# Outputs of the last two passes of each MoE layer combined by TensorE from SBUF; the overflow branch ahead of the passes; one comparison per pass index

## The chip, the core and the metric

The kernel runs on one core of a Trainium2 chip. Its five engines each work through a queue of their own: TensorE (PE, with its weight loads shown apart as PEld), VectorE (DVE), ScalarE (ACT), GpSimd (POOL) and SyncE (SP). Transfers run on 16 DMA engines and are issued from SP's and ACT's queues, and from POOL's queue where rows are picked by an index (indirect). The metric is the device time of one execution in microseconds.

## The reference

Two layers of a transformer over 256 latent and 256 context rows of width 1024. Each layer is attention, then a mixture of experts (MoE); the change touches the MoE and the lines around it. Cut to that:

```python
def moe(h, ...):                       # 16 experts in 4 groups, 2 experts per row
    s = jax.nn.sigmoid(h @ router_w); sel = s + router_bias
    ...                                # best group by its two best, then the top 2 of it
    w = take(s, idx); w = w / sum(w)
    act = silu(h @ w_gate[e]) * (h @ w_up[e]) * gates
    return sum_e act @ w_down[e]

x = layer_norm(ALPHA * x + g1 * attention(...), ln1_g, ln1_b)
y = moe(modulate(x, sh2, sc2), ...)
x = layer_norm(ALPHA * x + g2 * y, ln2_g, ln2_b)
```

Layer 0 does this for both streams (4 tiles of 128 rows), layer 1 for the latent rows alone (2 tiles). The output is the latent stream. All data are fp32.

## The kernel before

The MoE (`moe`) works in **passes**. A pass is a block of 128 row slots that belong to one to four experts (`unit_passes`: 11 passes in layer 0, 8 in layer 1). Routing on DVE gives each row two slots, one for each of its experts. The normalized rows `hx` are written to the memory table H; for each pass `route_index` builds a one-hot table `roh` on DVE, PE turns it into 128 row numbers `ridx`, and POOL fetches these rows from H (`xb<-H,ridx`). Then, per pass: PE turns the rows (`xbp`), `gate_up` multiplies them by gate and up weights (`pgu<-egu,xT`), `act` applies the activation (ACT `th`, DVE `ac`, PE `acp`, ACT `acT`), `down` gives the pass's output in PSUM (`y<-edn,acT`), and `rows_out` copies it to `yo` (DVE and ACT) and writes it to the memory table Y through ACT's queue. `down` of a pass stands one pass behind its `gate_up`.

Experts' weights are 3 MB each; SP loads them (`weight`, L1747) in pieces of 0.5 and 1 MB into pools of 11, 4 and 8 buffers, in the order of the passes. Which experts follow is read from DVE's table `metai`, except for two experts of layer 0 (table `early`) and the first group of layer 1, which are loaded ahead of the end of the routing.

At the end of a layer the rows come together. The **last** pass's output stays in PSUM, is multiplied by the gate vector g2 (`gated`, L1970, `ylast`) and is picked for each tile by a matmul with a one-hot table that carries the router's weights (`pcomb<-ylast,arena`, two matmuls a tile, each two rows of the trace). All other passes' outputs are picked from Y by POOL (`y_gather`, `yg<-Y,yslot`, two a tile), summed with the router's weights (`y_sum`: ACT L1875, DVE L1876), multiplied by g2 on POOL (`gate`, L1923), added to the residual (`add`, DVE L1963), and joined with `pcomb` (`combine`, DVE L1882). Behind the joins come the layer norm, and in layer 0 the first input projection of layer 1 (`pw`), whose weights `W1` are split in a high part (ACT CAST `whi<-wraw`, L1752) and a low part (POOL `wlo`, L1755 and L1759).

Rows beyond an expert's slots take the **overflow branch** (`tc.If(nov > 0)`, L1817), which stands behind `gate_up` of the second-to-last pass. With this data it is not taken. Each engine reads the flag and branches. On the way past it, SP waits until all transfers issued so far have landed, and raises the counters on which later reuses of the branch's buffers wait.

What sets the order on an engine is the order in which the code emits instructions, with priorities; inside `with self.ordered(last)` (the end of a layer) the order is as written.

Of the kernel before, what the change touches and what calls it, by code (L numbers as in the profile page):

```python
# [85 lines left out]
def shape_constants():  # L86
# [22 lines left out]
    route = np.zeros((DEPTH, 472), np.float32)  # L109
    for l in range(DEPTH):  # L110
        route[l, 0:256] = (e[None, :] < e[:, None]).reshape(-1)
        route[l, 256:384] = k
        route[l, 384:400] = e
        route[l, 400:408], route[l, 408:416] = slot_tables(l)
        route[l, 432:448] = 32 * e
        route[l, 448:452] = 4 * g
        route[l, 452:456] = g
        route[l, 456:472] = e % 4
# [10 lines left out]
NOROW = OVER + 5 * P  # L129
# [25 lines left out]
class Net:  # L155
# [160 lines left out]
    def consts2(self):  # L316
# [25 lines left out]
        self.Y = self.dr.tile([NOROW + P, D], F32, name="Y")  # L342
# [198 lines left out]
    def w_half(self, l, segs, h, wide=False):  # L541
# [660 lines left out]
    def out_proj(self, l, xs, tiles):  # L1202
# [18 lines left out]
        with self.ordered():  # L1221
            for n, k in enumerate(toks):
                p = toks[n - 1] if n else None
                self.out_half(k, W, 0, "AB")
                if n:
                    self.rows_turn(p)
                    self.rows_affine(p, 0)
                    self.rows_scale(p)
                    if n > 1:
                        self.route_gate(toks[n - 2])  # L1230
                    self.rows_affine(p, 1)
                    self.rows_sums(p, 3)
                    if n == 3:
                        self.route_choose(0)
                    if n == T - 1:
                        self.rows_scale(p)
                self.out_half(k, W, 0, "CD")
                self.rows_residual(k, 0)
                if n:
                    if n < T - 1:  # L1240
                        self.rows_scale(p)
                    self.rows_modulate(p)
                    if n == 3:
                        self.route_gates(0)
                    if n == T - 1:
                        self.rows_shift(p)
# [4 lines left out]
                if n == 3:  # L1251
                    self.route_early()
# [22 lines left out]
            if T == 4:  # L1275
                run[1]()
            self.rows_shift(end)
# [165 lines left out]
    def route_start(self, T):  # L1443
# [3 lines left out]
        k = self.small.tile([P, 216], F32, name="rk", bufs=1)  # L1447
        src = self.I["k_route"][self.l:self.l + 1, :]
        self.nc.scalar.dma_start(k, src[:, 256:472].to_broadcast([P, 216]))
        self.nc.scalar.dma_start(self.arena[:, 0:256], src[:, 0:256].to_broadcast([P, 256]))  # L1450
        self.iota, self.iota16, self.m32 = (k[:, a:b] for a, b in ((0, 128), (128, 144), (176, 192)))
        self.tab8 = k[:, 144:160].rearrange("p (a b) -> p a b", a=2)
# [709 lines left out]
```

## Time and profile before

| | |
|---|---|
| median of 3 runs | 1018.45 us (1015.17 to 1018.92) |
| the profiled execution | 1018.93 us, its span 1017.2 us |
| busy share of the span | PE 82%, DVE 56%, ACT 33%, POOL 20% |
[...]
| memory traffic | 231.55 MB, mean 228 GB/s |
| layer 0: passes and end | 400 to 620 us |
| layer 1: passes and end | 852 to 1017 us |

Times in rows are from the span's start. A row gives an instruction or several alike in a run (`xN`), its length, and in brackets how long its engine had been idle before it and what ended the idle time. SPq and ACTq are the queues' own DMA issues. A window's PEclk is the granted TensorE clock as a share of full speed; DMA is the mean busy share of the 16 DMA engines.

### The profile page before, as it was taken

The page shows a single profiled execution, that of the slowest core. Times are in us where ns is not written, and L with a number is a line of the kernel's source. Part 1 is how long each engine was busy: PE and PEld are TensorE (multiplying, and loading weights), DVE is VectorE, ACT ScalarE, POOL GpSimd, SP SyncE. Part 2 cuts the span into 40 slices and gives each one's busy share as a digit, 9 for nine tenths or more (in the row PEclk, how much of TensorE's full clock was granted, in tenths as well). Part 3 has the DMA queues.
Part 4 walks back from the last instruction along what each step waited for, and adds up shares of the span by engine and source line. Part 5 has one row for each costly group of instructions (what it writes and reads, how often), then busy time and mean ns, then how long its engine had stood idle before and what let it go on. Part 6 is the DMA issues. An engine that isn't in the chain of part 4 may idle for free. (4 is left out here: it accounts for less than half of the span.)

```text
span 1017.2 us, 12760 instructions
## 1 busy us (share of the span) xinstructions
PE 839.1 (82%) x4268; PEld 454.3 (45%) x4268; DVE 564.6 (56%) x1540; ACT 332.2 (33%) x775; POOL 203.3 (20%) x207
## 2 busy tenths in 40 slices
PE   4899999999899964699997348899997995897871
PEld 2476555545356732233332115665663673333320
DVE  4466776667485687523212198687776669320115
ACT  2243554535353210011111227555555520110101
POOL 1422110003230111100000384322235011100003
PEclk9999999999999985799999868999998997899986
DMA  9863666464624187999997642244525287999953
GB/s 341 291 232 115 214 210 225 133 237 135 243 89 171 42 291 267 388 327 401 366 400 257 221 161 83 83 166 120 161 90 159 83 289 259 345 391 402 395 205 119
DMA packets 131738, 231.55 MB, mean 228 GB/s; under 512 B 10192, under 2 KB 91696, under 8 KB 127568
## 3 DMA queue, kind: packets, MB, share of 16 engines
q1 hardware_dynamic: 116352, 186.84, 52.5%
q10 hardware_dynamic: 10992, 28.07, 7.7%
q0 software_dynamic: 4320, 15.73, 4.2%
q8 instruction: 37, 0.61, 0.2%
q14 instruction: 37, 0.30, 0.1%
HBM read 216.40 MB, written 17.89 MB: 230 GB/s over the span
## 5 line engine op out<-in xcount | busy, mean ns | idle before, releaser
L1785 PE MATMUL pgu<-egu,xT 128*32 128x512 f32 (+2 forms) x752 | 163.5, 623 | 16.7 <-DMA egu<-in_exp_w_gate_dram 6.5
L264 PE MATMUL pw<-whi,xhi 128*128 128x512 f32 (+1 forms) x224 | 94.5, 423 | 4.8 <-ACT xhi L476 4.0
L1038 ACT ACTIVATE P<-S,nm 128x512 f32<-128x512 f32 (+1 forms) x120 | 73.2, 614 | 76.8 <-DVE nm L1027 56.4
L1785 PEld LDWEIGHTS pgu<-egu,xT 128*32 128x32 f32 (+2 forms) x752 | 49.1, 132 | 106.5 <-issue 104.9
L266 PE MATMUL pw<-whi,xlo 128*128 128x512 f32 (+1 forms) x224 | 90.3, 406 | 3.9 <-DVE xlo L527 3.4
L265 PE MATMUL pw<-wlo,xhi 128*128 128x512 f32 (+1 forms) x224 | 90.3, 404 | 0.0
L1793 DVE SCALAR_TENSOR_TENSOR ac<-th,pgu 128x256 f32<-128x256 f32 x19 | 8.0, 420 | 134.7 <-ACT th L1791 134.7
L1807 PE MATMUL y<-edn,acT 128*32 128x512 f32 (+2 forms) x376 | 73.2, 617 | 6.6 <-ACT acT L1799 6.6
L1027 DVE TENSOR_REDUCE nm<-S 128x1 f32<-128x512 f32 (+1 forms) x120 | 68.4, 595 | 15.5 <-PE S L1000 11.0
L264 PEld LDWEIGHTS pw<-whi,xhi 128*128 128x128 f32 x224 | 43.2, 193 | 32.3 <-issue 16.2
L1682 POOL DMA_INDIRECT xb<-H,ridx x18 | 17.5, 972 | 191.8 <-DVE roh L1671 71.8
L365 PE MATMUL adaacc<-adaw,cst 128*32 128x512 f32 x256 | 53.8, 605 | 0.0
L254 POOL TENSOR_TENSOR wolo<-woraw,wohi 128x512 fp32r<-128x512 f32 x32 | 41.0, 1309 | 48.9 <-ACT wohi L253 48.7
L266 PEld LDWEIGHTS pw<-whi,xlo 128*128 128x128 f32 x224 | 43.0, 192 | 14.0 <-DVE xlo L527 4.7
L1068 PE MATMUL PTp<-ident,P 128*128 128x128 f32 x320 | 46.6, 277 | 2.9 <-DVE P L1056 2.5
L265 PEld LDWEIGHTS pw<-wlo,xhi 128*128 128x128 f32 x224 | 42.9, 191 | 9.9 <-issue 1.6
L1068 PEld LDWEIGHTS PTp<-ident,P 128*128 128x128 f32 x320 | 36.0, 141 | 24.3 <-issue 15.7
L1791 ACT ACTIVATE th<-pgu 128x256 f32<-128x256 f32 x19 | 7.3, 383 | 121.2 <-PE pgu L1785 84.6
L1807 PEld LDWEIGHTS y<-edn,acT 128*32 128x32 f32 (+2 forms) x376 | 23.1, 129 | 49.0 <-issue 32.7
L1975 PE MATMUL pcomb<-ylast,arena 128*128 128x512 f32 x24 | 20.0, 984 | 29.7 <-DVE ylast L1970 29.7
L264 PE MATMUL pwo<-wohi,oT 128*128 128x512 f32 x96 | 38.9, 405 | 0.7 <-ACT oT L258 0.7
L1075 ACT COPY PT<-PTp 128x512 f32<-128x512 f32 (+1 forms) x60 | 30.9, 514 | 22.6 <-PE PTp L1068 19.1
(412 smaller groups left out, 1580.6 us busy)
## 6 DMA issues: line engine op xcount, KB each, us to landing
adaw<-in_w_ada_dram SPq DMA_DIRECT2D x32, 1024.0 KB
egu<-in_exp_w_gate_dram SPq DMA_DIRECT2D x64, 512.0 KB
egu<-in_exp_w_up_dram SPq DMA_DIRECT2D x64, 512.0 KB
edn<-in_exp_w_down_dram SPq DMA_DIRECT2D x26, 1024.0 KB
adaw<-in_w_ada_dram SPq DMA_DIRECT2D x32, 512.0 KB
wraw<-in_w_in_dram SPq DMA_DIRECT2D x20, 512.0 KB
Y<-yo ACTq DMA_DIRECT2D x17, 512.0 KB
woraw<-in_w_out_dram SPq DMA_DIRECT2D x8, 1024.0 KB
```

The costliest lines, as they stand in the source:

```text
L254: eng.tensor_sub(lo[:, s], src[:, s], hi[:, s].bitcast(F32))
L264: mm(out, a[0], b[0], start=start, stop=False)
L265: mm(out, a[0], b[1], start=False, stop=False)
L266: return mm(out, a[1], b[0], start=False, stop=stop)
L365: self.nc.tensor.matmul(acc[32 * j:32 * j + 32, :], self.cst[:, k if row is None else row, :], t[:, j, :], start=(k == 0), stop=stop)
L1027: nc.vector.tensor_reduce(t.nm[:, j:j + 1], t.S[j][:, :t.nk], axis=AX.X, op=OP.max, negate=True)
L1038: self.last_exp = nc.scalar.activation(t.P[:, j, :t.nk], t.S[j][:, :t.nk], AF.Exp, bias=t.nm[:, j:j + 1], accum_out=t.l[:, j:j + 1])
L1068: nc.tensor.transpose(t.pt[n][:, k, :], t.P[:, n, k * P:(k + 1) * P], self.ident)
L1075: (nc.vector.tensor_copy if t.kind != "A" and n == 0 else nc.scalar.copy)(out, t.pt[n][:, 0:nkt, :])
L1785: mm(ps[c:c + w, :], xT[:, kk, c:c + w], W[a][kk // 4][:, kk % 4, :], start=kk == 0, stop=kk == KT - 1)
L1807: mm(ys[n][c:c + w, :], aT[:, f, c:c + w], W[a][2][f][:, n * 512:(n + 1) * 512], start=f == 0, stop=f == 1)
L1975: nc.tensor.matmul(got[n].ps[c], self.pickT[:, n, :], yg[0 if i in LAT_TILES else 1][:, c, :], start=True, stop=True)
```

## The change

1. The outputs of the last **two** passes stay on the chip: `ylast` is now a tile of two passes, copied from PSUM by ACT (three of four halves) and DVE (one). The table that picks from it, `pickT`, covers 256 slots (two PE turns a tile instead of one) and is made one pass earlier. For the passes before these two, `y_gather` is issued one pass earlier; unused rows point at rows of zeros in Y.
2. For each tile PE adds up everything in PSUM: two matmuls of the identity with the sum of the gathered rows, then four of `pickT` with `ylast` (`mul`: 6 matmuls instead of 2). `join` applies g2 (DVE, from PSUM) and adds to the scaled residual. POOL's `gate`, DVE's `add` and `gated` are gone. `y_sum` (`total`) moves into the ordered end, two tiles ahead of its join.
3. The low part of `W1` is made by DVE in two subtractions instead of by POOL; the casts of the high part stand behind the copies of `ylast` in ACT's queue.
4. The overflow branch moves ahead of the passes (layer 0: behind the index of pass 0; layer 1: behind `gate_up` of pass 0). Its preparation (`route_over`) runs only inside it; a flag `anyi` is computed with four small DVE instructions.
5. The index of a pass is one comparison on DVE over 2·T·128 columns instead of 2·T over 128, with twice the small matmuls; index and fetch of pass 1 come before the turn of pass 0, and `route_gates`/`route_rest` behind `gate_up` of pass 0. One of layer 0's `hx` writes (`rows_shift(p)`) moves behind the routing's sums, and `rest` (what is left of the modulation vectors) behind pass 0's `gate_up`.

```diff
+            self.rows_shift(p)
             self.rows_shift(end)
             self.route_rank()
             self.route_rows()
             self.first = self.route_index(0) if T == 4 else self.picks()
-            self.route_gates(n0)
-            self.route_gates(n0)
             self.route_experts()
-            if T == 4:
-                rest()
-            self.route_over()
+        self.ada_end = rest if T == 4 else None
...
-            with self.tc.issue_after(self.last_gather.ins):
-                self.split2(hl[0], hl[1], t, 0, self.last_ah if h else None, self.late if h else None)
+            def split():
+                self.nc.scalar.copy(hl[0], t)
+                self.nc.vector.tensor_sub(hl[1], t, hl[0].bitcast(F32))
+            self.late.append(split)
...
+        rel = self.rows
+        if base:
+            rel = self.sm([P, 2, T], "rrel")
+            nc.vector.tensor_scalar(rel, self.rows, -float(base * P), None, op0=OP.add)
+        oh = self.pj.tile([P, 2, T, P], BF16, name="roh", tag="pj")
+        both = [P, 2, T, P]
+        nc.vector.tensor_tensor(oh, self.iota[:, None, None, 0:P].to_broadcast(both), rel[:, :, :, None].to_broadcast(both), OP.is_equal)
...
-        nov = self.meta(36, 20)
-        with self.tc.If(nov > 0, preferred_fallthrough_block=False):
+        some = self.meta(0, 1, self.anyi)
+        with self.tc.If(some > 0, preferred_fallthrough_block=False):
+            self.route_over()
...
-        oh = self.pj.tile([P, 2, P], F32, name="lastoh", tag="pjd", bufs=2)
+        oh = self.pj.tile([P, 2, 2 * P], F32, name="lastoh", tag="pj")
         for c in range(2):
             nc.vector.tensor_scalar(oh[:, c], self.iota, self.rel[:, c, n:n + 1], self.gab[:, c, n:n + 1], op0=OP.is_equal, op1=OP.mult)
-        nc.vector.tensor_add(oh[:, 0], oh[:, 0], oh[:, 1])
+        self.last_oh = nc.vector.tensor_add(oh[:, 0], oh[:, 0], oh[:, 1])
         pt = self.pt("lastp")
-        nc.tensor.transpose(pt[:, 0, :], oh[:, 0], self.ident)
-        nc.scalar.copy(self.pickT[:, n, :], pt[:, 0, :])
+        for b in range(2):
+            nc.tensor.transpose(pt[:, b, :], oh[:, 0, b * P:(b + 1) * P], self.ident)
+        nc.scalar.copy(self.pickT[:, n], pt[:, 0:2, :])
...
+        if T == 4:
+            self.overflow(l)
+        gather(1)
+        blocks, prev, got = {0: rows_of(0)}, None, []
         fetch(0)
         fetch(1)
-        gather(1)
         for p, (_, segs) in enumerate(plan):
             gather(p + 2)
             ps = self.gate_up(segs, W, blocks[p], self.pa("pgu"))
+            if p == 0:
+                if T == 2:
+                    self.overflow(l)
+                else:
+                    with self.behind(self.last_idx, self.last_mm):
+                        self.ada_end()
+                for n in range(0, T, 2):
+                    self.route_gates(n)
+                self.route_rest()
             if p < end:
                 blocks[p + 1] = rows_of(p + 1)
                 fetch(p + 2)
-            if prev:
-                finish(*prev)
+                if prev:
+                    finish(*prev)
+                prev = p, ps
+            if p == end - 2:
                 g2 = self.bc_ada(l, 2, 1, streams)
-                self.pickT = self.arena[:, 0:T * P].rearrange("p (t q) -> p t q", t=T)
+                self.pickT = self.h([P, T, 2, P], "pickT")
                 for n in range(T):
                     self.last_rows(n)
-            if p == end:
+            if p == end - 1:
                 got = [self.y_gather(n) for n in range(T)]
...
+        def total(n):
             if n < T:
-                stt(xs[tiles[n]], xs[tiles[n]], ALPHA, ygs[n], op0=OP.mult, op1=OP.add)
+                bag[n].y = self.y_sum(n, got[n])
...
+        def mul(n, i):
+            g = bag[n]
+            g.ps = [al("pcomb") for al in (self.pa, self.pw)]
             for c in range(2):
-                nc.vector.tensor_mul(yg[s][:, c, :], last_y[c], g2[:, s, c * 512:(c + 1) * 512])
-
-        def mul(n, i):
-            got[n].ps = [al("pcomb") for al in (self.pa, self.pw)]
+                nc.tensor.matmul(g.ps[c], self.ident, g.y[:, c * 512:(c + 1) * 512], start=True, stop=False)
+            for a in range(2):
+                for c in range(2):
+                    nc.tensor.matmul(g.ps[c], self.pickT[:, n, spot[a]], yl[:, a, c], start=False, stop=a == 1)
...
+        def join(n, i):
+            x, g = xs[i], bag[n]
+            g.tot = self.sm([P, 4], "restot", bufs=8)
             for c in range(2):
-                nc.tensor.matmul(got[n].ps[c], self.pickT[:, n, :], yg[0 if i in LAT_TILES else 1][:, c, :], start=True, stop=True)
-
-        def join(n, i):
-            x, g = xs[i], got[n]
-            g.tot = self.sm([P, 4], "restot", bufs=8)
-            self.combine(x, g.ps, g.tot)
+                h = slice(c * 512, (c + 1) * 512)
+                t = self.pj.tile([P, 512], F32, name="rest", tag="pj")
+                nc.vector.tensor_mul(t, g.ps[c], g2[:, 0 if i in LAT_TILES else 1, h])
+                stt(x[:, h], x[:, h], ALPHA, t, op0=OP.mult, op1=OP.add, accum_out=g.tot[:, c:c + 1])
+            nc.vector.tensor_tensor(g.tot[:, 2:3], g.tot[:, 0:1], g.tot[:, 1:2], OP.add)
...
         with self.ordered(last):
-            gated(streams[-1])
-            add(0)
+            acA, acB = self.act_rows(psA), self.act_rows(psB)
+            self.down(plan[end - 1][1], W, self.act_turn(acA), ysA)
+            total(0)
+            self.down(plan[end][1], W, self.act_turn(acB), ysB)
+            for c in range(2):
+                nc.scalar.copy(yl[:, 0, c], ysA[c])
+            split()
+            total(1)
+            nc.vector.tensor_copy(yl[:, 1, 0], ysB[0])
+            nc.scalar.copy(yl[:, 1, 1], ysB[1])
```

Where the order on the engines moves, three places. SP's queue in layer 0, around the end of the routing (`early` and `metai` are the tables from which SP reads the experts; the second `egu`, `edn` of a place is an expert's second half). Before:

```order
L1350 DMA H<-hx 128x1024
L1747 ISA
L1747 DMA egu<-in_exp_w_gate_dram 128x4x256
L1747 ISA
L1747 DMA egu<-in_exp_w_up_dram 128x4x256
L1747 ISA
L1747 DMA edn<-in_exp_w_down_dram 128x2x1024
L1850 TENSOR_LOAD metai
L1747 ISA
```

After:

```order
L1747 DMA egu<-in_exp_w_gate_dram 128x4x256
L1747 ISA
L1747 DMA egu<-in_exp_w_up_dram 128x4x256
L1747 ISA
L1747 DMA edn<-in_exp_w_down_dram 128x2x1024
L1847 TENSOR_LOAD anyi
L1813 COMPARE_AND_BRANCH
L1813 UNCONDITIONAL_BRANCH
...
L1813 UNCONDITIONAL_BRANCH
L1847 TENSOR_LOAD metai
L1747 ISA
L1747 DMA egu<-in_exp_w_gate_dram 128x4x256
```

The write of `hx` has left this place for one ahead of the loads (both of layer 0's last two `hx` writes stand there now), and between the early loads and the first read of `metai` stands the branch. Its block is left out here (row 67 to 487); it is skipped.

POOL's queue from pass 0's fetch to the end of layer 0. Before:

```order
L1682 DMA xb<-H,ridx 128x1024 x10
L1850 TENSOR_LOAD metai
L1817 COMPARE_AND_BRANCH
L1817 ISA
L1817 UNCONDITIONAL_BRANCH
L1682 DMA rxb<-H,ridx 128x1024 x5
L1817 UNCONDITIONAL_BRANCH
L1867 DMA yg<-Y,yslot 128x1024 x8
L1923 TENSOR_TENSOR yg<-yg,bc 128x1024 x3
L1759 TENSOR_TENSOR wlo<-wraw,whi 128x2048
L1923 TENSOR_TENSOR yg<-yg,bc 128x1024
L1755 TENSOR_TENSOR wlo<-wraw,whi 128x512
```

After:

```order
L1690 DMA xb<-H,ridx 128x1024
L1847 TENSOR_LOAD anyi
L1813 COMPARE_AND_BRANCH
L1813 ISA
L1813 UNCONDITIONAL_BRANCH
L1690 DMA rxb<-H,ridx 128x1024 x5
L1813 UNCONDITIONAL_BRANCH
L403 MEMSET adar 64x512
L1690 DMA xb<-H,ridx 128x1024 x10
L898 TENSOR_SCALAR wuq<-wuq,lcol 128x384
L899 TENSOR_SCALAR wuq<-wuq,lcol 64x384
L1865 DMA yg<-Y,yslot 128x1024 x8
L212 TENSOR_TENSOR lsr<-lsv,mhalf 128x1 x5
```

The branch stands behind the first fetch instead of behind the last, only two products for layer 1's `wuq` stand between the last fetch of rows and the gathers of the layer's end, and the products with g2 and the subtractions for `W1` are gone.

DVE's queue at the end of layer 0, from the last product of an activation to the first join (`y_5466`/`y_5525` are halves of the outputs of the second-to-last and the last pass before, `y_5458` of the last pass after). Before:

```order
L1794 SCALAR_TENSOR_TENSOR ac<-ac,pgu 128x256
L207 COPY yo<-y_5466 128x512
L1876 SCALAR_TENSOR_TENSOR yg<-yg,arena 128x1024 x2
L1970 TENSOR_TENSOR ylast<-y_5525,bc 128x512
L1876 SCALAR_TENSOR_TENSOR yg<-yg,arena 128x1024
L1970 TENSOR_TENSOR ylast<-y_5526,bc 128x512
L1963 SCALAR_TENSOR_TENSOR x<-x,yg 128x1024
L1876 SCALAR_TENSOR_TENSOR yg<-yg,arena 128x1024
L1963 SCALAR_TENSOR_TENSOR x<-x,yg 128x1024
L1882 SCALAR_TENSOR_TENSOR x,restot<-pcomb,x 128x512 x2
L1884 TENSOR_TENSOR restot<-restot 128x1
L237 TENSOR_SCALAR lnm<-restot 128x1
```

After:

```order
L1786 SCALAR_TENSOR_TENSOR ac<-ac,pgu 128x256
L1874 SCALAR_TENSOR_TENSOR yg<-yg,arena 128x1024
L556 TENSOR_TENSOR wlo<-wraw,whi 128x2048
L1874 SCALAR_TENSOR_TENSOR yg<-yg,arena 128x1024
L2030 COPY ylast<-y_5458 128x512
L1874 SCALAR_TENSOR_TENSOR yg<-yg,arena 128x1024
L1976 TENSOR_TENSOR rest<-pcomb,bc 128x512
L1977 SCALAR_TENSOR_TENSOR x,restot<-x,rest 128x512
L1976 TENSOR_TENSOR rest<-pcomb,bc 128x512
L1977 SCALAR_TENSOR_TENSOR x,restot<-x,rest 128x512
L1978 TENSOR_TENSOR restot<-restot 128x1
```

`ylast` is one copy of 512 columns, the two `add` are gone, a subtraction for `W1` over 128x2048 has come in ahead of the second sum, and a join is four instructions of 512 columns.

## Rows read from the trace of the kernel before

**Rows 1.** PE timeline, layer 0's passes: start, us, instruction, [idle <-releaser]:

```profile
419.09 1.97 PE L1724 MATMUL xbp<-ident,xb 128*128 128x128 f32 x8 [6.38 <-DMA xb<-H,ridx]
...
531.07 7.07 PE L1785 MATMUL pgu<-egu,xT 128*32 128x512 f32 x62
...
540.40 3.65 PE L1807 MATMUL y<-edn,acT 128*64 128x512 f32 x16 [0.46 <-ACT acT L1799]
...
548.26 1.92 PE L1785 MATMUL pgu<-egu,xT 128*64 128x512 f32 x2 [4.21 <-issue]
...
559.75 0.44 PE L1797 MATMUL acp<-ident,ac 128*128 128x128 f32 x2
```

**Rows 2.** window in layer 0's passes: busy by engine, PEclk, DMA share, GB/s:

```profile
425.00:455.00 30.00, 28.90 (x152) 10.80 (x149) 10.37 (x42) 3.85 (x8) 1.90 (x2) 0.99 0.96 330
```

**Rows 3.** SP's queue in layer 0: early, first and last loads:

```profile
388.88 0.46 SPq L1747 DMA_DIRECT2D edn<-in_exp_w_down_dram  x1
...
398.36 0.38 SPq L1747 DMA_DIRECT2D egu<-in_exp_w_gate_dram  x1
...
535.18 1.29 SPq L1747 DMA_DIRECT2D edn<-in_exp_w_down_dram  x1
...
556.50 0.94 SPq L547 DMA_DIRECT2D wraw<-in_w_in_dram  x2
```

**Rows 4.** DVE timeline, layer 0's routing: last one-hot instruction of pass 0:

```profile
393.95 0.35 DVE L1672 SCALAR_TENSOR_TENSOR roh<-rk,rrel,roh 128x128 bf16<-128x128 f32 x1
```

**Rows 5.** PE timeline, layer 0's end: both last down projections, two matmuls of pcomb:

```profile
564.13 5.34 PE L1807 MATMUL y<-edn,acT 128*32 128x512 f32 x32 [3.94 <-ACT acT L1799]
...
570.49 3.65 PE L1807 MATMUL y<-edn,acT 128*64 128x512 f32 x16 [0.66 <-ACT acT L1799]
...
603.17 3.52 PE L1975 MATMUL pcomb<-ylast,arena 128*128 128x512 f32 x4 [9.69 <-DVE ylast L1970]
```

**Rows 6.** a window between the first and the second join, columns as in group 2:

```profile
600.00:605.00 5.00, 1.83 (x2) 0.83 (x3) 4.88 (x12) 1.24 (x2) 3.48 (x2) 0.50 0.70 210
```

**Rows 7.** ACT timeline, layer 0's end:

```profile
561.63 1.90 ACT L1752 CAST whi<-wraw 128x2048 fp32r<-128x2048 f32 x1 [7.67 <-DMA wraw<-in_w_in_dram]
```

**Rows 8.** tile yg, 570 to 590: issues (min/median/max ns) and landing times:

```profile
L1867 POOL DMA_INDIRECT yg<-Y,yslot x8: 937/941/1292, 573.6 to 582.6; - x8
...
DMA to landing us min/median/max: 4.2/5.3/6.3
```

**Rows 9.** DVE timeline, layer 0's end:

```profile
580.22 1.28 DVE L1876 SCALAR_TENSOR_TENSOR yg<-yg,arena 128x1024 f32<-128x1024 f32 x1 [12.86 <-DMA yg<-Y,yslot]
...
594.53 5.51 DVE L1963 SCALAR_TENSOR_TENSOR x<-x,yg 128x1024 f32<-128x1024 f32 x1
...
599.97 0.68 DVE L1882 SCALAR_TENSOR_TENSOR x<-pcomb,x 128x512 f32<-128x512 f32 x1
...
605.03 1.22 DVE L1963 SCALAR_TENSOR_TENSOR x<-x,yg 128x1024 f32<-128x1024 f32 x1
...
619.87 0.68 DVE L1882 SCALAR_TENSOR_TENSOR x<-pcomb,x 128x512 f32<-128x512 f32 x1
```

**Rows 10.** windows of layer 1's passes, columns as in group 2:

```profile
880.00:885.00 5.00, 4.46 (x26) 1.92 (x24) 2.56 (x10) 1.34 (x3) 0.49 (x1) 1.00 0.63 188
885.00:960.00 75.00, 66.18 (x422) 26.46 (x420) 11.06 (x27) 9.25 (x19) 3.26 (x4) 0.98 1.06 394
```

**Rows 11.** SP's queue timeline, first load behind layer 1's routing:

```profile
855.45 0.40 SPq L1747 DMA_DIRECT2D egu<-in_exp_w_gate_dram  x1
```

**Rows 12.** PE timeline, layer 1's end:

```profile
985.90 3.65 PE L1807 MATMUL y<-edn,acT 128*64 128x512 f32 x16 [0.61 <-ACT acT L1799]
...
998.15 4.87 PE L1975 MATMUL pcomb<-ylast,arena 128*128 128x512 f32 x6 [7.54 <-DVE ylast L1970]
```

**Rows 13.** DVE timeline, layer 1's end: the first halves of both joins:

```profile
1002.31 0.68 DVE L1882 SCALAR_TENSOR_TENSOR x<-pcomb,x 128x512 f32<-128x512 f32 x1
...
1007.59 0.68 DVE L1882 SCALAR_TENSOR_TENSOR x<-pcomb,x 128x512 f32<-128x512 f32 x1
```

More of the change, by code (lines that the diff above doesn't have):

```diff
@@ L1460, in route_start @@
         self.yslot = self.small.tile([P, 2, 4], I32, name="yslot", bufs=1)
-        self.metai = self.small.tile([P, 48], I32, name="metai", bufs=1)
-        self.hx, self.pc = [], None
+        self.metai = self.small.tile([P, 16], I32, name="metai", bufs=1)
+        self.units = self.small.tile([P, 20], I32, name="units", bufs=1)
+        self.anyi = self.small.tile([P, 1], I32, name="anyi", bufs=1)
+        self.hx, self.pc, self.sg = [], None, {}
         if T == 2:
@@ L1625, in route_rows @@
         self.rows_of_choice()
+        self.over, most = ar(16), ar(1)
+        tt(self.over, self.pc[:, 64:80], self.cap, OP.subtract)
+        self.red(most, self.over, OP.max)
+        nc.vector.tensor_scalar(most, most, 0.0, 1.0, op0=OP.max, op1=OP.min)
+        nc.vector.tensor_copy(self.anyi, most)
     def rows_of_choice(self):
@@ L1707, in route_rest @@
         self.rel = ar(2, T)
-        ts(self.rel, self.rows, -float(self.last0), None, op0=OP.add)
-        end, nov, ev = ar(16), ar(1), ar(20)
-        tt(end, self.ou, self.ovs, OP.add)
-        b20 = [P, 20, 16]
-        t = self.spare.rearrange("p (a b) -> p a b", a=20)
-        tt(t, end[:, None, :].to_broadcast(b20), self.iota[:, 0:20, None].to_broadcast(b20), OP.is_le)
-        self.red(ev, t, OP.add)
-        ts(ev, ev, 15.0, None, op0=OP.min)
-        self.red(nov, self.ou, OP.add)
-        nc.vector.tensor_copy(self.metai[:, 16:36], ev)
-        nc.vector.tensor_copy(self.metai[:, 36:37], nov)
+        ts(self.rel, self.rows, -float(first), None, op0=OP.add)
     def block_turn(self, xb, xT):
@@ L1748, in weight @@
                                w[(bass.ds(e, 1), *idx)].rearrange("o p t n -> (o p) t n"))
-    def split2(self, hi, lo, src, cut, after, late=None):
-        with self.tc.issue_after(after.ins) if after else nullcontext():
-            self.nc.scalar.copy(hi, src)
-        n = src.shape[1]
-        if late is not None:
-            late += [lambda a=a: self.nc.gpsimd.tensor_sub(lo[:, a], src[:, a], hi[:, a].bitcast(F32)) for a in range(n)]
-            return
-        for eng, a, b in ((self.nc.vector, 0, cut), (self.nc.gpsimd, cut, n)):
-            if b > a:
-                eng.tensor_sub(lo[:, a:b], src[:, a:b], hi[:, a:b].bitcast(F32))
     def expert_raw(self, l, e):
@@ L1956, in moe @@
         xT = None if mod is None else self.alloc_xT()
-        got = [Bag() for _ in tiles]
+        yl = self.raw([P, 2, 2, 512], "ylast")
+        ysA, ysB = [self.pw("y2"), self.pw("y3")], [self.po("y0"), self.po("y1")]
+        bag = [Bag() for _ in tiles]
         last = {}
         stt = nc.vector.scalar_tensor_tensor
-        def add(n):
+        order = [b for b, _ in plan[-2:]]
+        spot = [order.index(b) for b in sorted(order)]
+        def total(n):
             if n < T:
-                stt(xs[tiles[n]], xs[tiles[n]], ALPHA, ygs[n], op0=OP.mult, op1=OP.add)
@@ L2101, in run @@
                     self.layer_load(l, nc.scalar)
-                self.layer_params(l)
+                with self.behind(self.last_oh, self.last_fetch):
+                    self.layer_params(l)
             fill = []
@@ L2119, in zero_fill @@
         jobs = []
-        for t, first, n in ((self.Y, OVER // P - 1, 7),):
+        for t, first, n in ((self.Y, NOROW // P, self.Y.shape[0] // P - NOROW // P),):
             for b in range(first, first + n, ZB):
```

154 lines of the change are left out of this document (65 added, 89 removed).

## The prediction

> **What bounds the kernel now.** I read the windows first, then each engine's timeline where the change cuts in. Layer 0's passes: PE is busy 28.9 of 30 us at the full clock, and the DMA engines have a share of 0.96 and move 330 GB/s meanwhile [rows 2]. So PE sets the pace there, with the weights close behind. PE stops in two places: 6.38 us ahead of pass 1's turn, for the fetched rows, and 4.21 us ahead of the last pass's products, which no transfer explains ("issue"): that is the overflow branch [rows 1]. Layer 1's passes: 394 GB/s and a DMA share of 1.06 through 75 us [rows 10]; the weights set the pace.
>
> The ends of the layers are chains with PE mostly idle. Layer 0: the last product of `gate_up` is done at 559.75 [rows 1], PE waits 3.94 us for `acT`, because ACT was held by a cast that waited 7.67 us for `W1` [rows 5, 7]; the last output is complete at 570.49 + 3.65 = 574.14 [rows 5]. Only then does POOL gather, 4.2 to 6.3 us to land each [rows 8]; then come the sums, the products with g2 on POOL, and residual additions that take DVE 5.51 us beside POOL, 1.22 us alone; the first join stands at 599.97, the fourth at 619.87 [rows 9]. That is 40.2 us from the end of `gate_up` to the first join, 25.8 of them behind the last output. Layer 1: last output at 985.90 + 3.65 = 989.55, `pcomb` at 998.15 after 7.54 idle [rows 12], joins at 1002.31 and 1007.59 [rows 13].
>
> **The change part by part.**
>
> *Routing and pass 1, layer 0.* Eight one-hot instructions of at most 0.35 us [rows 4] become one over 128x1024. The nearest row of that size is 1.28 us [rows 9], so -1.5; the `hx` instruction that moves into this chain is of the same size, +1.3; the flag adds four of the smallest. I take 0 for pass 0, with -2 and +2 as bounds. The index of pass 1 now follows at once, so its rows arrive during pass 0 and the 6.38 us go. Against this stands SP's barrier in the branch: SP goes on only when the second early expert has landed. Its last piece was issued at 388.88, and the first load behind the routing at 398.36 [rows 3]; 3 MB at the 394 GB/s of a full stretch [rows 10] take 7.6 us, so the barrier opens at about 397 to 399, then comes the read of `metai`. I take the load stream 2 us late, and 1 us for pass 0, whose second half of turned rows waits on ACT for the same counters. Bounds: 0, and 4. Sum -5.4.
>
> *Can the weights follow?* From 425 to 455 the engines moved 330 instead of 394 GB/s [rows 2, 10]: 30 x 64/394 = 5 us of transfer time to be had, since buffers come free earlier when PE is earlier. Less the 2 us of the barrier, that is about the 5 us that PE gains; more would not follow. I take the gain whole; as a bound half of it.
>
> *The last pass of layer 0.* Its turn was ready and the output of pass 8 done at 540.40 + 3.65 = 544.05; `gate_up` ended at 559.75, 15.7 us later [rows 1]. An undisturbed one takes 7.07 us for 31 of its 32 products and 1.04 for the first, 8.1 [rows 1]. So 7.6 us go: the branch, the turns of the one-hot tables and the restart behind them. These turns are twice as many now, one pass earlier, between products of an engine that is never idle there; I charge 2.4 us (bounds 1 and 4). So `gate_up` ends 5.4 + 7.6 - 2.4 = 10.6 us earlier, say 11: at 549. Bounds 5 and 15.
>
> *The end of layer 0* (T is the end of `gate_up`). ACT's cast no longer stands ahead of `acT`: `y` of pass 9 at T+1.4 and pass 10 by T+10 (3.65 us each at full clock, one small gap each [rows 5]); before it was T+14.4. The gathers of the first two tiles need Y up to pass 8, written while pass 10 multiplies; they land near T+4. A sum costs DVE 1.28 [rows 9], and ACT ahead of it about the same. The gathers of the third tile take over buffers of the first: issue near T+7, landing 5.3 later [rows 8], sum by T+15. On DVE, ahead of the first join, also stand a subtraction over 128x2048 (estimate 2.4, twice the 1.28 for 1024 columns less its fixed part) and one copy. On PE six matmuls replace two. Two matmuls (four trace rows) took 3.52 us at half clock [rows 5, 6], 1.76 each; PE comes out of `y` without a pause now, so I take the full clock, 0.9 each: 5.4 from T+10. Both chains meet at T+15 to T+16. So the first join comes 24 us earlier, counted from T.
>
> From there DVE sets the pace, as before: the four joins spanned 599.97 to 619.87, 19.9 us [rows 9]. Per tile a join gains two products from PSUM (0.68 each, as the join's own half [rows 13]) and loses the 1.22 us of `add` [rows 9]; two sums (1.28) and one subtraction (2.4) move in, a pair of products by g2 (1.28) moves out: 4 x 1.36 - 3 x 1.22 + 2.6 + 2.4 - 1.3 = +5.5, of which the sum of the third tile already stands ahead of the first join, and the first join's own two products come with its start: about +3. Sum for layer 0's end: -24 + 3 = -21. Bounds: -14 (PE at half clock: six matmuls cost 10.5, and the gathers 2 us later) and -24. PE's added 16 matmuls, 14 us, lie beside DVE; if DVE were not there they would still fit its 6 to 7 us per tile.
>
> [...] Of the eight gather issues the median took 0.94 us and the longest 1.29 [rows 8]; within their stretch, at 580.22, DVE ran a sum [rows 9]. [...]
>
> *Layer 1.* Ahead of the load stream DVE now has one more `hx` (1.28), two one-hot instructions over 128x512 (0.68 each by the row of that size [rows 13]) and the flag, and no gates (about 1): the first load, 855.45 [rows 11], comes up to 3 us later. Some comes back: 880 to 885 moved 188 instead of 394 GB/s [rows 10], 2.6 us of transfer time lost, in the stretch after pass 1 waited for its rows. I take +1.5 (bounds -1 and +4). For the branch behind the last passes I take nothing back, since the weights set the pace there [rows 10]. At the end the gathers are out of the chain: six matmuls at full clock from 989.6 end at 995, so the first join stands at about 995.5 instead of 1002.31; the second tile's six end at 1000.5, so the second join is at 1001 instead of 1007.59, less one product more in each (0.68) and 1 us since ACT's sum stands ahead of the last `acT`. I take -5 (bounds: -7; +3 with PE at half clock).
>
> Sum: -10.6 - 21 + 1.5 - 5 = -35 on the profiled execution's 1018.93 (span 1017.2, 1.7 us around it): 984. That run lies 0.5 above the median of 1018.45, so 983 to 984; I say **983**.
>
> **The rivals.**
> - *As summed, 973 to 992.* Chance 0.6.
> - [...] Chance 0.16.
> - *The weights do not follow in layer 0.* Then routing and branch give back most of 11 us: 990 to 994. For it the share of 0.96 in [rows 2]; against it the view of PE's waits in layer 0's passes names no weights. Chance 0.1.
> - *PE's added matmuls run at half clock*, at 10.5 us a tile against DVE's 7.5: +7 in layer 0, +8 in layer 1: 998. For it the half clock of [rows 6]; against it the engine works without a pause ahead of them. Chance 0.05.
> - *Slower: the barrier stands at the head of the weights.* In the old place SP issued nothing from 535.18 + 1.29 to 556.50 [rows 3], 20 us, at a time when nothing was wanted. If it held SP as long ahead of both layers' streams, 40 us would be added and the gain of pass 1 (5) lost: 1018.9 - 30 + 40 = 1029. It decides from about 15 us a layer. Against it: what is in flight there is 3 MB or less. Chance 0.06.
> - *It doesn't do what it says*: the next projection waits for something else (its weights, DVE's own work), and the joins' gain ends there: 1010 to 1020. Chance 0.03.
>
> **How the numbers follow.** The likeliest case gives 983. Leaving out the slower rival, the last and a little of the edges (2 in 10) gives 973 to 1000. A measurement of this kernel tells 0.5% (5 us) from no change. Faster holds the first four cases and part of the last: 0.92; the same 0.02; slower 0.06.
>
> **What would show it.** PE's wait ahead of pass 1's turn gone; no "issue" wait ahead of the last `gate_up`, and its end near 549; first load of layer 0's stream at 398 to 401; PE without a pause over 1 us from the last `gate_up` to the second tile's `pcomb`; first join 15 to 16 us after `gate_up`, joins 7 to 8 us apart; layer 1's first load at 857 to 859 less what layer 0 gained, its joins 5 to 6 us apart, the first 6 us behind the last output. The prediction is wrong if SP's first load behind a branch is over 10 us late, if `pgu` waits for `egu` in layer 0, if `yg` of the third tile ends the wait of the first join, or if the time won at a layer's end is lost ahead of the next projection.

## The result, and the profile after

| | us |
|---|---|
| before, median of 7 runs beside the changed kernel | 1016.29 (1014.97 to 1018.92) |
| changed, median of 7 runs | 1008.71 (1002.16 to 1011.28) |
| ratio | 0.992, 95% interval 0.989 to 0.995 |
| forecast | 983, range 973 to 1000 |
| profiled execution of the changed kernel | 1008.71, span 1006.6, mean granted clock 0.945 (before: 0.926) |

The kernel is faster, by 0.8% where 3.5% was forecast. The time lies outside the range. Spans are compared below: 1017.2 before, 1006.6 after, 10.6 us of a forecast 35.

PE's timeline after: start, length, instruction, [idle <-releaser]. The first nine rows are of layer 0, the last is of layer 1's pass 0.

```profile
404.72 0.35 PE L1683 MATMUL ridx<-tokv,roh 128*128 128x2 bf16 x8 [7.18 <-issue]
...
406.83 1.94 PE L1724 MATMUL xbp<-ident,xb 128*128 128x128 f32 x8 [1.75 <-DMA xb<-H,ridx]
...
418.42 0.63 PE L1724 MATMUL xbp<-ident,xb 128*128 128x128 f32 x4 [0.73 <-DVE adah L414]
...
419.20 7.09 PE L1774 MATMUL pgu<-egu,xT 128*64 128x512 f32 x32
...
554.76 10.00 PE L1774 MATMUL pgu<-egu,xT 128*64 128x512 f32 x30 [6.31 <-DMA egu<-in_exp_w_up_dram]
...
565.59 3.64 PE L1803 MATMUL y<-edn,acT 128*32 128x512 f32 x32 [0.46 <-ACT acT L1795]
...
571.17 3.65 PE L1803 MATMUL y<-edn,acT 128*64 128x512 f32 x16 [1.57 <-ACT acT L1795]
...
574.76 1.98 PE L1965 MATMUL pcomb<-yg,ident 128*128 128x512 f32 x4
...
576.58 3.60 PE L1968 MATMUL pcomb<-ylast,pickT 128*128 128x512 f32 x8
...
854.24 8.76 PE L1774 MATMUL pgu<-egu,xT 128*64 128x512 f32 x30 [7.14 <-issue]
```

Against [rows 1]: the 6.38 us ahead of pass 1's turn are gone (0.73 is left, for something else), but pass 0's turn now begins at 406.83 (before: 400.39), and ahead of it PE stands 7.18 us at the branch's new place ("issue", 404.72). The "issue" wait ahead of the last `gate_up` is gone too, and in its place stand 6.31 us for weights (`egu`). `gate_up` ends at 554.76 + 10.00 = 564.8, 5 us later than before, where 549 was forecast. Against [rows 5]: from there PE goes nearly without a pause through both down projections into `pcomb`, with one gap of 1.57 us, at a granted clock of 1.00 in 564 to 580 (1.98 for four trace rows, against 3.52 for four where [rows 6] give 0.50).

PE's waits in 420 to 570 (us in total, times, longest), the one line on weights:

```profile
PE pgu L1774 <- DMA egu<-in_exp_w_up_dram: 9.8, 2, 6.3
```

Before, this view had no line on weights. SP's queue after, layer 0 and then layer 1:

```profile
378.78 0.41 SPq L1747 DMA_DIRECT2D egu<-in_exp_w_gate_dram  x1
...
392.25 0.39 SPq L1747 DMA_DIRECT2D egu<-in_exp_w_gate_dram  x1
...
410.78 0.38 SPq L1747 DMA_DIRECT2D egu<-in_exp_w_gate_dram  x1
...
844.17 0.40 SPq L1747 DMA_DIRECT2D egu<-in_exp_w_gate_dram  x1
...
858.76 0.39 SPq L1747 DMA_DIRECT2D egu<-in_exp_w_gate_dram  x1
```

Against [rows 3, 11]: the first load behind the routing is at 410.78 instead of 398.36, 12.4 us late. Of layer 1's it is at 844.17 instead of 855.45. DVE's joins after, the first halves of the first and fourth join in layer 0 and of both in layer 1:

```profile
579.35 0.69 DVE L1976 TENSOR_TENSOR rest<-pcomb,bc 128x512 f32<-128x512 f32 x1
...
605.58 0.68 DVE L1976 TENSOR_TENSOR rest<-pcomb,bc 128x512 f32<-128x512 f32 x1
...
989.64 0.69 DVE L1976 TENSOR_TENSOR rest<-pcomb,bc 128x512 f32<-128x512 f32 x1 [4.29 <-PE pcomb L1968]
...
995.36 0.68 DVE L1976 TENSOR_TENSOR rest<-pcomb,bc 128x512 f32<-128x512 f32 x1
```

Against [rows 9, 13]: the first join comes 14.6 us behind `gate_up` (forecast 15 to 16), the fourth at 605.58 instead of 619.87; the last of layer 1 at 995.36 instead of 1007.59. And the windows of the passes, columns as in [rows 2]:

```profile
425.00:455.00 30.00, 28.20 (x161) 11.61 (x158) 8.46 (x19) 4.84 (x10) 1.87 (x2) 1.00 1.06 380
...
455.00:485.00 30.00, 28.81 (x157) 10.64 (x156) 8.54 (x22) 4.24 (x9) 2.16 (x3) 1.00 1.07 378
...
495.00:535.00 40.00, 38.32 (x210) 15.10 (x206) 10.65 (x32) 6.00 (x13) 4.35 (x4) 0.99 1.07 374
...
885.00:960.00 75.00, 62.37 (x378) 23.96 (x372) 13.63 (x35) 9.62 (x21) 2.81 (x3) 0.95 1.07 377
```

A window of layer 0 before:

```profile
455.00:485.00 30.00, 28.84 (x145) 11.20 (x143) 8.66 (x31) 4.23 (x9) 1.89 (x2) 1.00 1.06 400
```

The prediction had not considered this. The DMA engines' share is as high as in the best windows of before, or higher (1.06 to 1.07), yet they move 374 to 380 GB/s; before it was 400 in this window and 394 in the stretch of layer 1 [rows 10]. The engines are as busy and bring 4 to 6% less.

### The profile page after: what moved, and what is told of

Same layout as the page of the kernel before. It is cut to its first block, busy times and chain, and to the rows that moved or that the text cites. A ratio compares the mean times of both kernels' runs of the same rounds, so it can differ in the third digit from the quotient of the medians.

```text
span 1006.6 us, 12875 instructions
## 1 busy us (share of the span) xinstructions
PE 847.7 (84%) x4380; PEld 460.7 (46%) x4380; DVE 539.3 (54%) x1415; ACT 335.2 (33%) x779; POOL 175.5 (17%) x196
## 5 line engine op out<-in xcount | busy, mean ns | idle before, releaser
L1774 PE MATMUL pgu<-egu,xT 128*32 128x512 f32 (+2 forms) x752 | 165.6, 635 | 31.6 <-DMA egu<-in_exp_w_up_dram 24.3
L262 PE MATMUL pwo<-wohi,oT 128*128 128x512 f32 x96 | 39.0, 406 | 0.7 <-ACT oT L256 0.7
L264 PE MATMUL pwo<-wohi,oT 128*128 128x512 f32 x96 | 37.9, 395 | 0.0
```

The costliest lines, as they stand in the source:

```text
L262: mm(out, a[0], b[0], start=start, stop=False)
L264: return mm(out, a[1], b[0], start=False, stop=stop)
L1774: self.last_mm = mm(ps[c:c + w, :], xT[:, kk, c:c + w], W[a][kk // 4][:, kk % 4, :], start=kk == 0, stop=kk == KT - 1)
```

## The experiments

Three theories at first, and the expectations name them: **A**, the branch, which now stands ahead of the weights' stream and stops SP and PE there; **B**, the new order around the end of layer 0's routing; **C**, the lower transfer rate, whatever makes it. Ratios are to runs of the kernel before on the same chip; its medians there were 1015.9 to 1017.0, so medians of different chips are set against each other too.

**The kernel before, again** (no edit; a profile beside the next three).

> The kernel before, unchanged, for its rate of transfer beside the others on the same chip. If the rate in layer 0's passes belongs to the chip and the day, this run too shows some 375 to 385 GB/s between 455 and 485 us (398 to 400 in the first trace of before); if the change lowers it, 395 to 400 again. The time should be 1015 to 1019 us.

Measured: 1016.21, a single run. Its windows:

```profile
455.00:485.00 30.00, 28.16 (x148) 11.03 (x147) 9.99 (x35) 5.17 (x11) 1.88 (x2) 1.00 1.03 380
...
495.00:535.00 40.00, 38.19 (x210) 14.35 (x206) 7.15 (x18) 5.78 (x12) 1.88 (x2) 1.00 1.06 399
...
885.00:960.00 75.00, 66.73 (x420) 26.62 (x420) 10.82 (x27) 9.25 (x19) 2.81 (x3) 0.95 1.06 394
```

In the window that the expectation names, 455 to 485, the rate is 380 GB/s, which the expectation would put down to the chip and the day. But the share is 1.03 there, so the engines were less busy. Where the share is 1.06 the kernel before moves 394 to 399 again, and the changed one 374 to 380 at 1.06 to 1.07. At an equal share the low rate comes with the change.

**The branch late again, in both layers.**

```diff
-        if T == 4:
-            self.overflow(l)
...
-                if T == 2:
-                    self.overflow(l)
-                else:
+                if T == 4:
...
             if p == end - 1:
+                self.overflow(l)
                 got = [self.y_gather(n) for n in range(T)]
```

Inside the branch `route_rest` runs again and its rows have another buffer; `layer_params` of layer 1 is no longer held behind `last_oh`.

> The changed kernel with the overflow branch put back to where it was, behind gate_up of the second-to-last pass, in both layers (inside it the table of slots is worked out again; its turned rows take a buffer of another pool). All else stays. Theory A, the branch ahead of the passes holds SP until the early weights have landed and PE for 7 us: the first load behind layer 0's routing goes out at 400 to 402 us instead of 410.8, PE waits under 3 us in all for weights in layer 0, PE does not stop 7 us in layer 1's pass 0, and the time is 989 to 997. Theory B, the new order around the end of the routing is late by itself (early loads at 378.8 instead of 369.3, both hx writes ahead of the second expert): SP is free earlier, but the engines are still busy with the early weights; PE waits 5 us or more for weights and the time is 999 to 1005. Theory C, the weights come at a lower rate than before and set the pace whatever stands ahead of them: PE waits stay at 8 to 10 us in layer 0 and the time is 1004 to 1010.

Measured: 1008.79 (1007.03 to 1009.54), ratio to before 0.992 [0.989, 0.995]. The stream of layer 0 starts 7.4 us earlier than in the changed kernel, and the rate stays low (a row of SP's queue, then windows as above):

```profile
403.39 0.37 SPq L1747 DMA_DIRECT2D egu<-in_exp_w_gate_dram  x1
```

```profile
455.00:485.00 30.00, 28.82 (x156) 10.76 (x158) 8.68 (x23) 4.23 (x9) 1.89 (x3) 1.00 1.07 378
...
495.00:535.00 40.00, 38.29 (x216) 14.98 (x216) 9.95 (x27) 6.92 (x16) 1.88 (x2) 1.00 1.07 378
...
885.00:960.00 75.00, 59.93 (x345) 21.32 (x341) 9.79 (x24) 8.56 (x18) 1.88 (x2) 0.91 1.07 375
```

The end of layer 0, PE and ACT:

```profile
549.07 8.56 PE L1774 MATMUL pgu<-egu,xT 128*64 128x512 f32 x32 [6.98 <-DMA egu<-in_exp_w_gate_dram]
...
563.91 0.66 ACT L1783 ACTIVATE th<-pgu 128x256 f32<-128x256 f32 x2 [21.19 <-SPq L1813]
...
565.35 0.66 PE L1793 MATMUL acp<-ident,ac 128*128 128x128 f32 x2 [7.72 <-DVE ac L1786]
```

PE waits 6.98 us ahead of the last `gate_up`. The profile puts that down to weights, but the branch now stands there, so its own stop lies in the same wait and the two cannot be told apart. Then PE waits 7.72 us for the activation, since ACT goes on only when SP is past the branch's barrier (21.19 us, SPq L1813). So the late branch costs about the same in sum, by another wait, and A's 989 to 997 do not come.

**Without the branch** (the work of experts with more than one tile is left out; not shown: `route_rest` moves from pass 0 to the turn in which `pickT` is made).

```diff
-        if T == 4:
-            self.overflow(l)
...
-                if T == 2:
-                    self.overflow(l)
-                else:
+                if T == 4:
```

> The changed kernel without the overflow branch (rows beyond an expert's slots would be lost; with this data there are none). It bounds what the branch costs at any place. Theory A: 984 to 993, and no idle time of PE put down to issue at a pass. Theory B: 996 to 1003, PE waiting for weights in layer 0 as in the changed kernel or a little less. Theory C: 1002 to 1010.

Measured: 998.84 (997.67 to 1000.43), ratio 0.982 [0.979, 0.985]; 378 GB/s in 495 to 535, 375 in layer 1, and PE waits 6.0 us for weights in layer 0. Having a branch costs 10 us, and its absence does not bring the rate back. The time lies in the range given for B, not in those for A and C; what speaks for C here is the rate, and B is not refuted by this run.

**The branch late in layer 0 alone** (the first edit above, under `T == 4` only).

> The branch put back in layer 0 alone; in layer 1 it stays behind gate_up of pass 0. Theory A: two thirds of the gain of putting back both, 995 to 1001; layer 1's PE still stops 7 us in pass 0 and SP's second group of loads still waits for it. Theory B: 1002 to 1007. Theory C: as the changed kernel within 3 us, 1006 to 1011.

Measured: 1010.78 (1009.25 to 1011.59), ratio 0.993 [0.991, 0.996], 378 GB/s. Nothing is won by the place in layer 0. The low rate is what all three kernels have in common, so the next runs ask what makes it; B was not tried by itself.

**Where C comes from.** The change makes the first pool, `small`, larger: `rk` from 216 to 308 columns, two new tiles, a smaller `metai`. The pools lie one behind another in SBUF, so every tile of the later pools starts 384 bytes higher in a partition. The start addresses in the two programs:

```
tile                before                         after
small               32288 (rk)                     32288 (rk)
egu, edn, wraw,     34816, 43008, ... 149504       35200, 43392, ... 149888
adaw, woraw         (all multiples of 512)         (all 384 past one)
```

I made two theories of it: *address* (transfers into tiles that start off a boundary are slower) and its rival, that the rate falls for anything else in the change. An unused tile in `small` moves the addresses of all later pools, those of tiles that only engines use too, and adds one small memset on POOL; nothing else changes. In the kernel before:

```diff
         k = self.small.tile([P, 216], F32, name="rk", bufs=1)
+        self.pad = self.small.tile([P, 96], F32, name="pad", bufs=1)
+        self.nc.gpsimd.memset(self.pad, 0.0)
```

> The kernel before with nothing changed but an unused tile of 384 bytes a partition in the first pool, so that every weight tile starts 384 bytes past a multiple of 512, as in the changed kernel (before: on one). Theory address: the transfers into SBUF fall from 394-400 GB/s to 375-380 in 455-535 and in layer 1, PE begins to wait for weights late in layer 0, and the time rises by 5 to 12 us, to about 1022-1029. Rival (the rate falls for something else in the change: branch, order, tables in memory): rate 394-400, no wait for weights, time 1017 within 3.

Measured: 1021.07 (1019.12 to 1026.07), ratio 1.0044 [1.0023, 1.0065]. Its windows, and PE's wait for weights in layer 1:

```profile
455.00:485.00 30.00, 28.20 (x143) 10.81 (x141) 9.50 (x33) 4.82 (x10) 1.89 (x2) 1.00 1.06 384
...
495.00:535.00 40.00, 38.18 (x210) 14.32 (x206) 7.16 (x18) 5.78 (x12) 1.87 (x2) 1.00 1.07 379
...
885.00:960.00 75.00, 62.80 (x408) 23.92 (x405) 10.37 (x26) 8.87 (x18) 2.81 (x3) 0.98 1.06 376
```

```profile
PE pgu L1787 <- DMA egu<-in_exp_w_up_dram: 9.9, 6, 5.4
```

The rate falls as in the changed kernel, at the same share. In layer 1 PE's waits for `egu` up-weights grow from 6.0 to 9.9 us. In layer 0 none appears, and the time rises by 4 us only, less than expected. That the weights have enough lead there is argued, not tried.

The same tile with 32 columns (128 bytes) in the changed kernel puts the starts back on multiples of 512.

> The changed kernel with an unused tile of 128 bytes a partition in the first pool, so that the weight tiles start on multiples of 512 again. Theory address: 394-400 GB/s in layer 0 and 390-395 in layer 1, PE's waits for weights in layer 0 (9.8 us) fall below 5, the time falls by 6 to 12 us to 996-1003, which still leaves 10 us or more of the branch that the forecast lacked. Rival: 375-380 GB/s as before the pad, 1008 within 3.

Measured: **994.37** (992.77 to 998.33), ratio to before 0.978 [0.975, 0.981], 14.3 us below the changed kernel, more than the 6 to 12 expected. Windows; then PE's last `gate_up` and its down projection in layer 0 and `gate_up` of layer 1's pass 0; then the fourth join of layer 0 and the last join:

```profile
425.00:455.00 30.00, 28.20 (x166) 11.31 (x168) 9.68 (x23) 4.81 (x10) 1.87 (x2) 1.00 1.06 400
...
455.00:485.00 30.00, 28.82 (x152) 10.52 (x144) 7.71 (x19) 3.85 (x8) 2.81 (x3) 1.00 1.06 399
...
885.00:960.00 75.00, 60.81 (x357) 23.85 (x354) 10.25 (x25) 8.25 (x18) 3.92 (x5) 0.95 1.05 394
```

```profile
544.25 8.75 PE L1776 MATMUL pgu<-egu,xT 128*64 128x512 f32 x30 [4.05 <-DMA egu<-in_exp_w_up_dram]
...
553.83 3.64 PE L1805 MATMUL y<-edn,acT 128*32 128x512 f32 x32 [0.46 <-ACT acT L1797]
...
843.95 9.36 PE L1776 MATMUL pgu<-egu,xT 128*64 128x512 f32 x30 [6.40 <-issue]
```

```profile
595.44 0.69 DVE L1978 TENSOR_TENSOR rest<-pcomb,bc 128x512 f32<-128x512 f32 x1 [0.80 <-PE pcomb L1970]
...
980.28 0.68 DVE L1978 TENSOR_TENSOR rest<-pcomb,bc 128x512 f32<-128x512 f32 x1
```

The rate is that of the kernel before, `gate_up` of layer 0 ends at 553.0, 11.8 us earlier than without the padding, and the last join is 15.1 us earlier. The address theory holds; its rival would have left 377 and 1008.

Without the branch and with the padding (the overflow work left out again):

> The changed kernel without the overflow branch (the work for experts with more than one tile is left out), with the 128 bytes of padding. Theory address and branch as two causes that add up: 10 us below the padded kernel, 986-993, near the forecast of 983. Theory that the branch alone matters: 998 as without padding.

Measured: 986.62 (985.33 to 988.74), ratio 0.970 [0.967, 0.974]. PE at the end of layer 0, then the same two joins:

```profile
541.23 7.03 PE L1776 MATMUL pgu<-egu,xT 128*64 128x512 f32 x30
...
556.78 5.35 PE L1805 MATMUL y<-edn,acT 128*64 128x512 f32 x16 [3.69 <-ACT acT L1797]
```

```profile
594.12 0.69 DVE L1974 TENSOR_TENSOR rest<-pcomb,bc 128x512 f32<-128x512 f32 x1 [1.16 <-PE pcomb L1966]
...
971.75 0.68 DVE L1974 TENSOR_TENSOR rest<-pcomb,bc 128x512 f32<-128x512 f32 x1
```

Two causes that add up: 14.3 for the addresses, 7.8 for the branch. `gate_up` ends at 548.3, where 549 was forecast. Of the branch's 7.8 us only 1.3 are seen at layer 0's fourth join (595.44 against 594.12); the other 7 come in layer 1 (980.28 against 971.75), where PE stands 6.40 us in pass 0.

**Which boundary counts.** The kernel before with 64 columns (256 bytes) of padding, and with 16 (64 bytes), a single run each.

> The kernel before with 256 bytes a partition of unused tile: the weight tiles start 256 bytes past a multiple of 512. If 256 is the step that counts, 394-400 GB/s in 455-535 as before; if 512 is, 375-380 as with 384.

Measured: 1016.63; in 455 to 485 it moves 386 GB/s at a share of 1.04. The window 495 to 535:

```profile
495.00:535.00 40.00, 38.18 (x210) 14.42 (x206) 7.16 (x18) 5.79 (x12) 1.88 (x2) 1.00 1.06 399
```

> The kernel before with 64 bytes a partition of unused tile. If any start off a multiple of 256 costs the same: 375-380 GB/s in 455-535, as with 384 bytes. If only part of it does: between 380 and 395.

Measured: 1025.46, a single run; 383 GB/s at 1.06 in 455 to 485. The window 495 to 535:

```profile
495.00:535.00 40.00, 38.18 (x210) 14.41 (x206) 7.15 (x18) 5.78 (x12) 1.87 (x2) 1.00 1.06 376
```

In this window a start 256 bytes past a multiple of 512 costs no rate, and 64 bytes past costs as much as 384 (which is 128 past a multiple of 256): 376 and 379 against 399. By these three starts the step is 256.

Both starts cost 5 to 6% of the rate (379 and 376 of 399), so these windows show no difference between 64 and 128 bytes past the boundary. Why a start off it costs rate is not shown by any run.

**The padded kernel with the branch late in both layers.**

> The changed kernel with 128 bytes of padding, and with the branch back in the turn before the last in both layers. In the padded kernel (994.4) the branch costs 7.8 us, nearly all of it in layer 1 (last gate_up 961.1 against 952.6 without it), where PE stands 6.4 us in pass 0 and SP's next loads wait for PE. Theory that the place matters (an early stop holds up the weights, a late one does not): 988-991. Theory that PE's stop of 6 to 7 us is paid wherever it stands: 994 within 3, as in the two unpadded kernels (1008.8 against 1008.7).

Measured: 994.25 (990.04 to 994.58), ratio 0.977 [0.975, 0.980]. Again nothing is won in sum. The next kernel shows that two differences cancel here.

**Padded, late in layer 1 alone.**

> As the kernel before in this list, but the branch late in layer 1 alone; in layer 0 ahead of the passes. Where the early branch of layer 0 is nearly free (595.4 against 594.1 at its fourth join) and the late one of layer 1 is cheaper than 8 us: 987-991. Where PE's stop is paid in full in layer 1 anywhere: 993-996.

Measured: **990.69** (988.71 to 991.44), ratio 0.975 [0.973, 0.977]: the best kernel here that leaves nothing out, 4 us below the padded one. PE's waits for weights in layer 1's passes:

```profile
PE pgu L1776 <- DMA egu<-in_exp_w_up_dram: 13.7, 4, 6.5
```

PE's stop in pass 0 is gone, and half of the branch's price with it; 4.1 us over the kernel without a branch stay. The waits for weights look longer than with the early branch (11.2). But the longest stands ahead of the last `gate_up`, at the branch's late place:

```profile
947.35 9.72 PE L1776 MATMUL pgu<-egu,xT 128*64 128x512 f32 x32 [6.47 <-DMA egu<-in_exp_w_up_dram]
```

In the padded kernel without a branch PE waits 4.5 us for weights within this same `gate_up` (3.04 and 1.44). So the stop of the late branch lies in large part over a wait that is there anyway; how much of the 6.47 us it makes is not separated.

The four kernels of the change with padding give the price by layer, as the time of layer 0's fourth join and the time from there to the last join (us, one profiled execution each):

| branch | fourth join, layer 0 | from there to the last join |
|---|---|---|
| none | 594.12 | 377.6 |
| ahead in both layers | 595.44 | 384.8 |
| late in both | 599.71 | 381.7 |
| ahead in layer 0, late in layer 1 | 596.80 | 381.0 |

So with the full rate the place does count, the opposite way in the two layers: late costs 3 to 4 us more in layer 0 and 3 to 4 less in layer 1, and late in both comes out as ahead in both. The two kernels with the branch ahead in layer 0 differ by 1.4 us there, so these are rough. In the kernels without padding this does not show: from the fourth join to the last join they take 388.3 without a branch, 389.8 with it ahead in both layers and 389.8 with it late in both.

## Why the prediction was wrong

The step that failed is **"Can the weights follow?"**. It took the rate of the kernel before, 394 GB/s in a full stretch, as given for the changed one, and asked only for free transfer time. The rate itself fell by 4 to 6%, since the tiles that the weights land in had moved off a multiple of 256 bytes. This is shown in both directions: padding gives the changed kernel 14.3 us back, and costs the kernel before 4.2. The diff had the widened `rk`, and I read it for its columns, not for its bytes. With the rate restored the time, 994.4, lies inside the range; without it, outside. My rival "the weights do not follow in layer 0" named the wait that came (9.8 us in layer 0), but for a late stream and at the old rate, at 990 to 994. The padded kernel's 994.4 is near that by chance: it has 4.1 us of such a wait, but 7.8 us of it are the branch, nearly all in layer 1.

A second step failed, **the branch at its new place**. The forecast read PE's 4.21 us of "issue" as the branch and counted them as won [rows 1], and charged nothing for PE's stop where the branch now stands; there it is 7.2 us in layer 0 and 7.1 in layer 1, and having a branch costs 8 to 10 us in all. Two of the prediction's own signs of being wrong came true: SP's first load behind a branch is over 10 us late, and `pgu` waits for `egu` in layer 0.

The other steps, by the padded kernels where the rate would hide them:

- *Routing and pass 1*, forecast -5.4. The 6.38 us are gone as told, but the stream was to be 2 us late and is 12.4 late; pass 0's first products start 6.6 us later (408.91 against 402.29). Up to `gate_up` of pass 1 the kernel gains 2 us unpadded, 4 padded (421.17 before, 419.20, 417.08). The branch is about 8 of the 12 us (first load 403 without it), the rest is a routing that ends 3 us later and early loads that start at 378.78 instead of 369.33. Mis-sized.
- *The last pass*, forecast -7.6 + 2.4 and an end at 549: 548.3 in the padded kernel without a branch, 553.0 with it, of which 4.05 are its one wait for weights. Right.
- *The end of layer 0*, forecast -21 from `gate_up` on: the fourth join stood 60.1 us behind it before [rows 1, 9], 40.8 after: -19.3. Right in sum, the full clock of PE too (1.00 in 564 to 580). Its two parts missed in opposite directions: the first join -25.6 for -24 (14.6 us behind `gate_up`, 40.2 before), the span of the four joins 26.2 instead of 19.9, +6.3 for +3. One gather issue, from 574.55 on, took 2.49 us, the others 0.95 to 1.00, and DVE ran a subtraction of 2.29 us from 573.93 on; landing rose to 7.9 us:

```profile
L1865 POOL DMA_INDIRECT yg<-Y,yslot x8: 947/947/2490, 562.7 to 577.3; - x8
...
DMA to landing us min/median/max: 4.3/6.3/7.9
```

  The long issue lies beside that subtraction; whether the one held up the other is not shown. ACT waited only 0.21 us for the third tile's rows, and DVE's sum of that tile (577.93) and the first join (579.35) waited for nothing: late gathers of the third tile, the case given a chance of 0.16, did not happen.
- *Layer 1's start*, forecast +1.5: layer 1 began 14.0 us earlier (its selection on DVE at 832.17, before 846.18), its first load only 11.3: +2.7, within the bounds of -1 and +4.
- *Layer 1's passes*, "for the branch I take nothing back": true, and incomplete. At its new place it stops PE for 7.14 us, SP's next loads wait 9.2 us for PE's buffers (844.17, then 858.76), and in the padded kernels this is not regained: 8.5 us less 1.3 between those with and without it. In the changed kernel itself the price lies in the other layer: 7.0 us at layer 0's fourth join (605.58, and 598.60 without a branch), 1.5 behind it. The slower rival, SP held for 15 us or more by the branch, did not happen (ahead of layer 0's stream SP issues nothing for 14.0 us, and for 6.8 without a branch); a stop of PE at the branch's new place was in none.
- *Layer 1's end*, forecast -5: from the last `gate_up` (980.45 before, 976.16 after) to the last join 27.1 before, 19.2 after: -7.9, somewhat beyond its bound of -7.

So, read in the padded kernels where rate or branch would hide them, the terms of the sum held within some 3 us each but for two, 14 us of rate and 8 us of branch: 983 + 14 + 8 = 1005 is near the 1008.7 measured, and with both taken away the kernel takes 986.6.

Open: theory B was not tried by itself, so whether the 7.6 us that the padded kernel's early loads are still late (376.92 against 369.33) cost the 4.1 us of waits is argued only. Nor was it tried which of the weights, `adaw`, `wraw` or the experts', lose how much of the 14.3 us.

## What to carry to other kernels

When a change alters the size of a tile in an early pool, work out the start of every tile that transfers land in, before and after: a few hundred bytes there moved all the weights' starts, and no line of the diff that touches a weight shows it. In the profile it reads as fewer GB/s at the same DMA share (374 to 380 instead of 394 to 400, at 1.06 to 1.07). What a lower rate costs differs from kernel to kernel: the same 5% cost 4 us in the kernel before and 14 in the changed one. I put this down to the lead of the transfers, since the changed kernel's stream starts 12 us later; that was not tried by itself. For a branch, ask what stands at its place: with the full rate it was cheaper ahead of the passes in layer 0, and in layer 1 late (by 3 to 4 us each), where PE waited for weights anyway.

## What the hardware showed that was not expected

- Transfers from memory into SBUF tiles that start 64 or 384 bytes past a multiple of 512 ran at 374 to 384 GB/s, those into tiles that start on one at 394 to 401, both at a busy share of 1.05 to 1.07. In 495 to 535 the two starts cost alike (376 and 379), and 256 bytes past cost nothing (399).
- A branch over a block that is skipped stopped PE with nothing in the profile that it waited for: for 7.18 us in layer 0 and 7.14 in layer 1 of the changed kernel, 6.40 in layer 1 of the padded one, 6.33 in layer 0 of the padded one with the branch late, and 4.21 in layer 0 of the kernel before. In the two kernels without a branch no such wait stands in 380 to 600 and 830 to 1000. What makes the stop is not separated by any run here.
